# Row sums of a 16384 x 1024 matrix: the first 2048 rows on 64 partitions, the last 2048 as one group

## The chip, the cores and the metric

The kernel runs on one core of a Trainium2 chip. The metric is the device time of one execution in microseconds (us), as the median of several runs. The core has a vector engine (DVE in the profile), a scalar engine (ACT), a GpSimd engine (POOL), a tensor engine that this kernel leaves idle, a sync engine (SP) that only issues transfers, and 16 DMA engines that carry the transfers between the memory outside (DRAM) and the buffer on the core, which has 128 partitions.

## The reference

```
batch, seq, dim = 32, 512, 1024
x: (32, 512, 1024) float32, normally distributed
return np.sum(x, axis=-1).astype(np.float32)        # (32, 512)
```

So 16384 rows of 1024 numbers (4 KB each, 64 MB in all) are read, and one sum for each row (64 KB in all) is written.

## The kernel before

**Tiling.** The rows are cut into eight groups of 2048. A group puts 16 consecutive rows (`BIG = 16`) on each of the 128 partitions: that is the view `x_g[g, p, j, d]` (L120). One partition's share of a group is therefore 64 KB that lie in one piece in DRAM. Input tiles hold a whole group, and the pool has three of them (L133), so the load of a fourth tile waits until the sums over the first one are done.

**Sums.** `vec` (L140) is one instruction of the vector engine that sums all the rows of a tile on each partition. `halves` (L153) is another form for one row: it adds the two halves of the row and sums the result. `act` (L166) has the scalar engine copy one row into a tile nobody reads, with the row's sum on the side. All sums land in the tile `sums`, one column per row of a partition.

**The helper `rows(t, a, n, j, n_act, pairs)`** (L177) loads `n` rows per partition with one transfer on SP's queue and gives the last `n_act` of them to the scalar engine and the others to the vector engine, as one `vec` or, with `pairs`, as one `halves` per row.

**Order of the work.** The schedule is manual: each engine does its instructions in the order in which they are written.

1. The first 7 rows per partition of the *last* group (`FIRST = 7`, L199), 3.5 MB, summed by one `vec`. This is the very first transfer: `issue_first_load_at_entry` (L10) moves the first load of SP's queue ahead of the barrier with which the program starts.
2. Groups 0 to 5, each with one load of 8 MB and one `vec`. The load of group 1 is held (`hold`, L145, adds a wait) until the first 7 rows have been summed.
3. Group 6 with one load; its rows are shared, 9 for `halves` and 7 for `act`.
4. The other 9 rows per partition of the last group in falling pieces: 6 rows, 2 rows, and one row that is itself cut at column 560 (`pieces = (560, 464)`). The two parts of that row are loaded into neighbouring places (`part`, `whole`); the sum of the first part is written into a column ahead of the second part, so that the second `halves` gives the sum of the row.
5. Two stores. The sums of groups 0 to 6 go out on the scalar engine's queue, held until the transfer of 2 rows (`two`) has landed. The sums of the last group go out on SP's queue after everything (L227).

`order_waits` (L31) puts the waits of an instruction in order, and `wait_for_the_store_at_the_clear` (L55) has the last store awaited by GpSimd's last clearing of semaphores instead of by SP.

Of the kernel before, what the change touches and what calls it, by code (L numbers as in the profile page):

```python
# [100 lines left out]
@with_exitstack  # L101
def kernel(
    ctx: ExitStack,
    tc: tile.TileContext,
    x: bass.AP,
    out: bass.AP,
):
    nc = tc.nc
    nc.at_finalize(issue_first_load_at_entry)
    nc.at_finalize(order_waits)  # L110
    nc.at_finalize(wait_for_the_store_at_the_clear)
    fp32 = mybir.dt.float32
    P = 128
    batch, seq, dim = x.shape
    rows = batch * seq
    J = rows // P
    BIG = 16


    x_g = x.flatten_outer_dims().rearrange("(g p j) d -> g p j d", p=P, j=BIG)  # L120
    out_v = out.rearrange("b s -> (b s)").rearrange("(g p j) -> p g j", p=P, j=BIG)

    def rows_from(j, n):
        return x_g[j // BIG, :, j % BIG : j % BIG + n, :]

    last = J // BIG - 1
    FIRST = 7
    pieces = (560, 464)  # L130

    with (
        tc.tile_pool(name="in", bufs=3) as inpool,  # L133
        tc.tile_pool(name="unread", bufs=4, space=bass.MemoryType.PSUM) as upool,
        tc.tile_pool(name="stage", bufs=1) as stpool,
        tc.manual_schedule(),
    ):
        sums = stpool.tile([P, J], fp32)

        def vec(dst, src):  # L140
            return nc.vector.tensor_reduce(  # L141
                out=dst, in_=src, axis=mybir.AxisListType.X, op=mybir.AluOpType.add
            )

        def hold(inst, until, reason):  # L145
            tc.add_manual_dep(
                inst.ins,
                until.ins.name,
                mybir.DependencyInfo(mybir.DependencyClass.Sync, mybir.DependencyReason.DATA),
                reason=reason,  # L150
            )

        def halves(dst, src):  # L153
            n = src.shape[-1] // 2
            return nc.vector.tensor_tensor_reduce(  # L155
                out=src[:, :n],
                in0=src[:, :n],
                in1=src[:, n:],
                scale=1.0,
                scalar=0.0,  # L160
                op0=mybir.AluOpType.add,
                op1=mybir.AluOpType.add,
                accum_out=dst,
            )

        def act(dst, src, n):  # L166
            unread = upool.tile([P, dim], fp32)
            nc.scalar.activation(  # L168
                out=unread[:, :n],
                in_=src,  # L170
                func=mybir.ActivationFunctionType.Copy,
                accum_out=dst,
            )

        sums_of = []

        def rows(t, a, n, j, n_act, pairs=False):  # L177
            nv = n - n_act
            block = t[:, a * dim : (a + n) * dim].rearrange("p (n d) -> p n d", d=dim)
            load = nc.sync.dma_start(out=block, in_=rows_from(j, n))  # L180
            if pairs:
                for q in range(nv):
                    sums_of.append(halves(sums[:, j + q : j + q + 1], block[:, q, :]))
            else:
                sums_of.append(vec(sums[:, j : j + nv], block[:, :nv, :]))
            for q in range(nv, n):
                act(sums[:, j + q : j + q + 1], block[:, q, :], dim)
            return load

        def store(eng, g0, g1):  # L190
            return eng.dma_start(
                out=out_v[:, g0:g1],
                in_=sums[:, g0 * BIG : g1 * BIG].rearrange("p (g j) -> p g j", j=BIG),
            )


        j = last * BIG
        t = inpool.tile([P, BIG * dim + 4], fp32)
        rows(t, 0, FIRST, j, 0)  # L199
        first = sums_of[-1]  # L200
        for g in range(last):
            t = inpool.tile([P, BIG * dim + 4], fp32)
            if g < last - 1:
                load = rows(t, 0, BIG, g * BIG, 0)
            else:
                rows(t, 0, BIG, g * BIG, 7, pairs=True)
            if g == 1:
                hold(load, first, "no descriptors of later loads while the first ones start")

        t = inpool.tile([P, BIG * dim + 4], fp32)  # L210
        rows(t, FIRST, 6, j + FIRST, 2, pairs=True)
        two = rows(t, FIRST + 6, 2, j + FIRST + 6, 1, pairs=True)
        a = BIG - 1

        j += a
        c, width = pieces
        whole = t[:, a * dim + c : BIG * dim + 2]
        nc.vector.memset(whole[:, width + 1 :], 0.0)  # L220
        part = t[:, a * dim : a * dim + c]
        nc.sync.dma_start(out=part, in_=rows_from(j, 1)[:, 0, :c])  # L222
        nc.sync.dma_start(out=whole[:, 1 : width + 1], in_=rows_from(j, 1)[:, 0, c:])
        hold(store(nc.scalar, 0, last), two, "its packets come behind those of the loads")
        halves(whole[:, :1], part)
        halves(sums[:, j : j + 1], whole)
        store(nc.sync, last, last + 1)  # L227


# [28 lines left out]
```

## Time and profile before

| what | value |
|---|---|
| time, median of 3 runs | 161.67 us (161.61 to 161.68) |
| span of the profiled execution, first to last instruction | 159.9 us |
| median time less that span (the profiled execution's own time is not given separately) | 1.8 us |
| vector engine busy | 120.6 us, 75%, 40 instructions |
| scalar engine busy | 12.0 us, 8%, 21 instructions |
| read from DRAM / written | 67.11 MB / 0.07 MB, 420 GB/s over the span |
| SP's queue (q1): packets, MB, share of the 16 DMA engines' time | 1872, 67.12, 97.7% |
| the scalar engine's queue (q10) | 912, 0.06, 0.4% |
| all packets; of these under 512 B / 2 KB / 8 KB | 2784; 1248 / 1376 / 1504 |

How to read it: the DMA engines are busy for nearly the whole span and the others are not, so what the kernel can lose or win lies where the DMA engines are not yet, or no longer, at work. A packet is one piece that one DMA engine moves. A load of a whole group is 128 packets of 64 KB, one for each partition, and 16 further packets of a few bytes that report its completion. The counts come out so: 12 loads of 128 packets are 1536, the stores move 1024 packets of 64 B, and 14 transfers report with 16 packets each (224); 1024 + 224 is the 1248 under 512 B, and with 1536 the whole 2784.

### The profile page before, as it was taken

Reading aid. Unit: us, or ns where it says so; the run is one execution under the profiler, and the core shown is the slowest. Engines: PE = TensorE matmul, PEld = TensorE weight load, DVE = VectorE, ACT = ScalarE, POOL = GpSimd, SP = SyncE. Lnnn points to the kernel's source line nnn. Section 1 sums busy time; section 2 is a strip of 40 time slices with the busy share of each in tenths; the row PEclk is TensorE's granted clock in tenths of the full one; section 3 lists DMA queues with packets and bytes.
Section 4 is the critical chain, followed back from the end, with each engine's and each line's share of the span. In section 5 each row is a group of like instructions: output and inputs, shape, how many; then the busy total and the mean of one; then the engine's idle time right before and its main releaser. Section 6 shows DMA issues by size and latency. Waiting matters only on the chain.

```text
span 159.9 us, 132 instructions
## 1 busy us (share of the span) xinstructions
DVE 120.6 (75%) x40; ACT 12.0 (8%) x21; POOL 0.2 (0%) x4
## 2 busy tenths in 40 slices
DVE  0029600499985999779995899949999499994955
ACT  3000000000000000000000000000000000003993
POOL 0000000000000000000000000000000000000000
DMA  8899899799699699699699699799898996996994
GB/s 308 380 492 525 361 426 525 328 459 525 295 492 525 262 525 525 262 525 525 262 525 508 279 525 476 312 525 410 377 525 361 426 525 262 525 525 289 400 384 124
DMA packets 2784, 67.18 MB, mean 420 GB/s; under 512 B 1248, under 2 KB 1376, under 8 KB 1504
## 3 DMA queue, kind: packets, MB, share of 16 engines
q1 hardware_dynamic: 1872, 67.12, 97.7%
q10 hardware_dynamic: 912, 0.06, 0.4%
HBM read 67.11 MB, written 0.07 MB: 420 GB/s over the span
## 4 chain that ended last, share of the span: by engine, by line
DMA 71%; DVE 27%; SPq 1%; issue 0%; DVEq 0%
DMA t<-in_x_dram 71%; DVE sums L141 26%; SPq L180 0%; SPq L222 0%; DVE t L155 0%; DVEq L253 0%
## 5 line engine op out<-in xcount | busy, mean ns | idle before, releaser
L141 DVE TENSOR_REDUCE sums<-t 128x16 f32<-128x16384 f32 (+1 forms) x7 | 110.9, 15848 | 33.4 <-DMA t<-in_x_dram 33.4
L168 ACT ACTIVATE unread<-t 128x1024 f32<-128x1024 f32 x10 | 10.1, 1013 | 144.7 <-DMA t<-in_x_dram 144.7
L155 DVE CUSTOM_DVE_ANT_0 t<-t 128x512 f32<-128x512 f32 (+2 forms) x16 | 9.6, 654 | 4.1 <-DMA t<-in_x_dram 4.0
L168 ACT ACTIVATION_READ_ACCUMULATOR unread<-t 128x1 f32 x10 | 1.9, 188 | 0.0
L168 ACT ACT_TABLE_LOAD x1 | 1.3, 1283 | 0.8 <-PEq L242 0.8
L155 DVE DVE_READ_ACCUMULATOR2_ANT sums<- 128x1 f32 x15 | 1.2, 81 | 0.0
L242 POOL MEMSET const-bfloat16-1.0<- 128x1 bf16 x1 | 0.1, 102 | 0.0
L242 POOL MEMSET const-uint8-127<- 128x1 uint8 x1 | 0.1, 102 | 0.0
L242 POOL MEMSET const-float32-1.0<- 128x1 f32 x1 | 0.1, 99 | 0.0
L242 POOL MEMSET const-float32-0.0<- 128x1 f32 x1 | 0.1, 98 | 0.2 <-issue 0.2
L155 DVE DVE_READ_ACCUMULATOR2_ANT t<- 128x1 f32 x1 | 0.1, 83 | 0.0
L220 DVE MEMSET t<- 128x1 f32 x1 | 0.1, 59 | 0.0
## 6 DMA issues: line engine op xcount, KB each, us to landing
t<-in_x_dram SPq DMA_DIRECT2D x1, 3584.0 KB, 11.0
t<-in_x_dram SPq DMA_DIRECT2D x1, 3072.0 KB, 28.9
t<-in_x_dram SPq DMA_DIRECT2D x1, 1024.0 KB, 31.0
t<-in_x_dram SPq DMA_DIRECT2D x1, 280.0 KB, 31.2
t<-in_x_dram SPq DMA_DIRECT2D x1, 232.0 KB, 31.3
t<-in_x_dram SPq DMA_DIRECT2D x7, 40.8
out_dram<-sums ACTq DMA_DIRECT2D x1, 56.0 KB, 2.1
out_dram<-sums SPq DMA_DIRECT2D x1, 8.0 KB, 1.4
```

The costliest lines, as they stand in the source:

```text
L141: return nc.vector.tensor_reduce(out=dst, in_=src, axis=mybir.AxisListType.X, op=mybir.AluOpType.add)
L155: return nc.vector.tensor_tensor_reduce(out=src[:, :n], in0=src[:, :n], in1=src[:, n:], scale=1.0, scalar=0.0, op0=mybir.AluOpType.add, op ...
L168: nc.scalar.activation(out=unread[:, :n], in_=src, func=mybir.ActivationFunctionType.Copy, accum_out=dst,)
L220: nc.vector.memset(whole[:, width + 1 :], 0.0)
L242: nc = _bacc.Bacc("TRN2", target_bir_lowering=False, num_devices=1)
```

## The change

The rows that used to be group 0 (the first 2048) are now read in another shape. They are put on the 64 partitions 32 to 95 in two "lines" of 1024 rows, again 16 consecutive rows per partition (view `x_s[l, q, j, d]`). Line 0 comes with four loads ("quarters"), the r-th of which takes the partitions 32 + r, 36 + r, 40 + r and so on: 16 partitions, 1 MB, each. Line 1 comes with one load of 64 partitions, which is held until the first quarter has landed. Of each line the vector engine sums the partitions 32 to 63 with one `vec`, and the scalar engine the partitions 64 to 95 with 16 `act`. The load of group 1 is held until the fourth quarter has landed.

The last group is no longer begun at the start. It comes at the end, whole, in pieces of 8, 5, 2 and 1 rows per partition, the one row cut as before. Of the 8 rows the scalar engine gets 3, of the 5 rows 2, of the 2 rows 1.

`sums` gets 16 columns more, since the two lines take 16 columns each on half of the partitions. Their sums are written by a store of their own on the scalar engine's queue, ahead of that of groups 1 to 6.

```diff
-    last = J // BIG - 1
-    FIRST = 7
+    LOW, HALF, Q = 32, 64, 32
+    x_s = x.flatten_outer_dims()[: P * BIG].rearrange("(l q j) d -> l q j d", l=2, j=BIG)
+    out_s = out.rearrange("b s -> (b s)")[: P * BIG].rearrange("(l q j) -> q l j", l=2, j=BIG)
+    last = G - 1
...
-        sums = stpool.tile([P, J], fp32)
+        sums = stpool.tile([P, J + BIG], fp32)
+        def at(g):
+            return (g + 1) * BIG
...
+        def line(t):
+            return t[LOW : LOW + HALF, : BIG * dim].rearrange("p (n d) -> p n d", d=dim)
+
+        def sum_line(t, c):
+            block = t[:, : BIG * dim].rearrange("p (n d) -> p n d", d=dim)
+            a = slice(LOW, LOW + Q)
+            vec(sums[a, c : c + BIG], block[a])
+            a = slice(LOW + Q, LOW + HALF)
+            for q in range(BIG):
+                act(sums[a, c + q : c + q + 1], block[a, q, :], dim, a)
...
-        j = last * BIG
         t = inpool.tile([P, BIG * dim + 4], fp32)
-        rows(t, 0, FIRST, j, 0)
-        first = sums_of[-1]
-        for g in range(last):
+        quarters = [
+            nc.sync.dma_start(out=line(t)[r::4], in_=x_s[0, r::4]) for r in range(4)
+        ]
+        sum_line(t, 0)
+        t = inpool.tile([P, BIG * dim + 4], fp32)
+        second = nc.sync.dma_start(out=line(t), in_=x_s[1])
+        hold(second, quarters[0], "no descriptors of later loads while the first ones start")
+        sum_line(t, BIG)
+
+        for g in range(1, last):
             t = inpool.tile([P, BIG * dim + 4], fp32)
             if g < last - 1:
-                load = rows(t, 0, BIG, g * BIG, 0)
+                load = rows(t, g, 0, BIG, 0)
             else:
-                rows(t, 0, BIG, g * BIG, 7, pairs=True)
+                rows(t, g, 0, BIG, 7, pairs=True)
             if g == 1:
-                hold(load, first, "no descriptors of later loads while the first ones start")
+                hold(load, quarters[3], "no descriptors of later loads while the first ones start")
 
         t = inpool.tile([P, BIG * dim + 4], fp32)
-        rows(t, FIRST, 6, j + FIRST, 2, pairs=True)
-        two = rows(t, FIRST + 6, 2, j + FIRST + 6, 1, pairs=True)
+        rows(t, last, 0, 8, 3, pairs=True)
+        rows(t, last, 8, 5, 2, pairs=True)
+        two = rows(t, last, 13, 2, 1, pairs=True)
...
-        hold(store(nc.scalar, 0, last), two, "its packets come behind those of the loads")
+        first = nc.scalar.dma_start(
+            out=out_s,
+            in_=sums[LOW : LOW + HALF, : 2 * BIG].rearrange("p (l j) -> p l j", j=BIG),
+        )
+        hold(first, two, "its packets come behind those of the loads")
+        hold(store(nc.scalar, 1, last), two, "its packets come behind those of the loads")
         halves(whole[:, :1], part)
-        halves(sums[:, j : j + 1], whole)
+        halves(sums[:, at(last) + a : at(last) + a + 1], whole)
         store(nc.sync, last, last + 1)
```

The helper `rows` now takes the group and the row in it instead of two offsets, and `act` takes the partitions it works on.

More of the change, by code (lines that the diff above doesn't have):

```diff
@@ L117 @@
     BIG = 16
+    G = J // BIG
     x_g = x.flatten_outer_dims().rearrange("(g p j) d -> g p j d", p=P, j=BIG)
     out_v = out.rearrange("b s -> (b s)").rearrange("(g p j) -> p g j", p=P, j=BIG)
-    def rows_from(j, n):
-        return x_g[j // BIG, :, j % BIG : j % BIG + n, :]
-    last = J // BIG - 1
-    FIRST = 7
+    LOW, HALF, Q = 32, 64, 32
+    x_s = x.flatten_outer_dims()[: P * BIG].rearrange("(l q j) d -> l q j d", l=2, j=BIG)
+    out_s = out.rearrange("b s -> (b s)")[: P * BIG].rearrange("(l q j) -> q l j", l=2, j=BIG)
+    last = G - 1
     pieces = (560, 464)
@@ L164, in halves, with act @@
             )
-        def act(dst, src, n):
+        def act(dst, src, n, on=slice(None)):
             unread = upool.tile([P, dim], fp32)
             nc.scalar.activation(
-                out=unread[:, :n],
+                out=unread[on, :n],
                 in_=src,
@@ L173, in act, with rows @@
             )
-        sums_of = []
-        def rows(t, a, n, j, n_act, pairs=False):
+        def rows(t, g, j, n, n_act, pairs=False):
             nv = n - n_act
-            block = t[:, a * dim : (a + n) * dim].rearrange("p (n d) -> p n d", d=dim)
-            load = nc.sync.dma_start(out=block, in_=rows_from(j, n))
+            block = t[:, j * dim : (j + n) * dim].rearrange("p (n d) -> p n d", d=dim)
+            load = nc.sync.dma_start(out=block, in_=x_g[g, :, j : j + n, :])
+            c = at(g) + j
             if pairs:
                 for q in range(nv):
-                    sums_of.append(halves(sums[:, j + q : j + q + 1], block[:, q, :]))
+                    halves(sums[:, c + q : c + q + 1], block[:, q, :])
             else:
-                sums_of.append(vec(sums[:, j : j + nv], block[:, :nv, :]))
+                vec(sums[:, c : c + nv], block[:, :nv, :])
             for q in range(nv, n):
-                act(sums[:, j + q : j + q + 1], block[:, q, :], dim)
+                act(sums[:, c + q : c + q + 1], block[:, q, :], dim)
             return load
+        def line(t):
[7 more added lines that the diff above has]
+                act(sums[a, c + q : c + q + 1], block[a, q, :], dim, a)
         def store(eng, g0, g1):
@@ L192, in store @@
                 out=out_v[:, g0:g1],
-                in_=sums[:, g0 * BIG : g1 * BIG].rearrange("p (g j) -> p g j", j=BIG),
+                in_=sums[:, at(g0) : at(g1)].rearrange("p (g j) -> p g j", j=BIG),
             )
-        j = last * BIG
         t = inpool.tile([P, BIG * dim + 4], fp32)
-        rows(t, 0, FIRST, j, 0)
-        first = sums_of[-1]
-        for g in range(last):
+        quarters = [
[7 more added lines that the diff above has]
+        for g in range(1, last):
             t = inpool.tile([P, BIG * dim + 4], fp32)
             if g < last - 1:
-                load = rows(t, 0, BIG, g * BIG, 0)
+                load = rows(t, g, 0, BIG, 0)
             else:
-                rows(t, 0, BIG, g * BIG, 7, pairs=True)
+                rows(t, g, 0, BIG, 7, pairs=True)
             if g == 1:
-                hold(load, first, "no descriptors of later loads while the first ones start")
+                hold(load, quarters[3], "no descriptors of later loads while the first ones start")
         t = inpool.tile([P, BIG * dim + 4], fp32)
-        rows(t, FIRST, 6, j + FIRST, 2, pairs=True)
-        two = rows(t, FIRST + 6, 2, j + FIRST + 6, 1, pairs=True)
+        rows(t, last, 0, 8, 3, pairs=True)
+        rows(t, last, 8, 5, 2, pairs=True)
+        two = rows(t, last, 13, 2, 1, pairs=True)
         a = BIG - 1
-        j += a
         c, width = pieces
@@ L221 @@
         part = t[:, a * dim : a * dim + c]
-        nc.sync.dma_start(out=part, in_=rows_from(j, 1)[:, 0, :c])
-        nc.sync.dma_start(out=whole[:, 1 : width + 1], in_=rows_from(j, 1)[:, 0, c:])
-        hold(store(nc.scalar, 0, last), two, "its packets come behind those of the loads")
+        nc.sync.dma_start(out=part, in_=x_g[last, :, a, :c])
+        nc.sync.dma_start(out=whole[:, 1 : width + 1], in_=x_g[last, :, a, c:])
+        first = nc.scalar.dma_start(
[4 more added lines that the diff above has]
+        hold(store(nc.scalar, 1, last), two, "its packets come behind those of the loads")
         halves(whole[:, :1], part)
-        halves(sums[:, j : j + 1], whole)
+        halves(sums[:, at(last) + a : at(last) + a + 1], whole)
         store(nc.sync, last, last + 1)
```

## The prediction

> **What bounds the kernel now.** I read the page first, then the vector engine's timeline, the busy times by stretch, the chain that ended last, and the start once more in short stretches.
>
> The vector engine's timeline (start, duration, what, in brackets the idle time before it and what ended it):
>
> ```profile
> 11.03 7.62 DVE L141 TENSOR_REDUCE sums<-t 128x7 f32<-128x7168 f32 x1 [11.03 <-DMA t<-in_x_dram]
> 30.34 17.22 DVE L141 TENSOR_REDUCE sums<-t 128x16 f32<-128x16384 f32 x1 [11.69 <-DMA t<-in_x_dram]
> 49.69 17.22 DVE L141 TENSOR_REDUCE sums<-t 128x16 f32<-128x16384 f32 x1 [2.14 <-DMA t<-in_x_dram]
> ```
>
> Every reduce waits for its load. They follow one another by 19.35 us and take 17.22, so a group of 8 MiB costs 19.35 us of transfer (433.5 GB/s) and the engine has 2.13 us to spare in each. The stretches say the same of the DMA engines (columns: stretch, length, busy DVE, ACT, POOL with counts, clock, DMA share, GB/s):
>
> ```profile
> 11.00:30.30 19.30, 7.62 (x1) 0.00 (x0) 0.00 (x0) 1.00 1.00 435
> 88.40:107.70 19.30, 17.22 (x1) 0.00 (x0) 0.00 (x0) 1.00 1.00 435
> 146.50:159.90 13.40, 9.66 (x33) 10.71 (x20) 0.00 (x0) 1.00 0.82 328
> ```
>
> The share is 1.00 in the middle. Time is lost only at the two ends. Of the chain that ended last (start, length, what) the ends matter:
>
> ```profile
> 0.00 11.01 DMA t<-in_x_dram
> 11.01 0.02 issue
> ...
> 126.33 31.29 DMA t<-in_x_dram
> 157.62 0.07 issue
> 157.69 0.40 DVE t L155
> ```
>
> 64 MiB at 19.35 us per 8 MiB are 154.80 us, and the last load lands at 157.62: 2.82 us are lost up to there. The first load, 7/16 of a group, should take 8.47 us and lands at 11.01, so 2.54 of the 2.82 lie at the start, and 0.28 in all the rest. After the landing come 2.26 us (last half sum, store, clearing) up to 159.88. The median is 161.67, 1.79 more than the span. I make the sum against the span and add 1.79.
>
> Now the start (packets are counted in the stretch where they begin; one is 28672 bytes here):
>
> ```profile
> 0.00:1.00 1.00, 0.00 (x0) 0.22 (x1) 0.20 (x4) 1.00 0.00 0
> 1.00:1.10 0.10, 0.00 (x0) 0.10 (x1) 0.00 (x0) 1.00 6.40 1720
> 1.10:1.30 0.20, 0.00 (x0) 0.20 (x1) 0.00 (x0) 1.00 3.79 1004
> 1.30:1.60 0.30, 0.00 (x0) 0.30 (x1) 0.00 (x0) 1.00 0.92 287
> 1.60:2.60 1.00, 0.00 (x0) 0.46 (x1) 0.00 (x0) 1.00 0.00 0
> 2.60:2.80 0.20, 0.00 (x0) 0.00 (x0) 0.00 (x0) 1.00 2.32 1004
> 2.80:3.05 0.25, 0.00 (x0) 0.00 (x0) 0.00 (x0) 1.00 2.39 1032
> 4.70:5.30 0.60, 0.00 (x0) 0.00 (x0) 0.00 (x0) 1.00 1.85 765
> ```
>
> GB/s times length over 28672 gives packets: 6 + 7 + 3 = 16, one for each DMA engine, beginning anywhere between 1.0 and 1.6; then 7 + 9 = 16 second ones between 2.6 and 3.05. Share times length times 16 over the count gives their mean duration: 1.71, 1.73 and 1.47 us for the first packets by the time they begin (1.67 over all), 1.06 for the second ones. The 16 packets of 4.70 to 5.30 took 1.11. So a first packet costs 0.61 us too much, the last engine is on its second packet only at 3.05, which is as if it had begun at 3.05 - 1.06 = 1.99 and lost nothing, and some 0.1 us more goes in the packets up to 6.5 (in the stretches 3.65 to 4.15, 4.70 to 5.30 and 5.80 to 6.50 the mean excess is 0.02, 0.05 and 0.01). 1.99 + 0.1 = 2.09; the other 0.45 of the 2.54 lie between the last data and the report of the landing.
>
> **The change part by part.**
>
> *The first load.* 16 packets of 64 KB instead of 128 of 28 KB: one per DMA engine. It removes nothing that must be transferred. It can only move the two losses above: when the last engine begins, and how long its first packet takes beyond its bytes. Before, 128 descriptors are written for the first load and, issued at 0.78 us, 128 more for group 0 while the first packets run. After, it is 16 and then 48 (the three other quarters, at 328 ns to some 440 ns per issue on SP, from 0.78 to about 2 us). Nothing in the trace shows a load of 16 packets, so I bound it. Best: the last engine begins at 1.0, when the first one did, with the excess of the late starters, 1.47 - 1.06 = 0.41: 1.41 in place of 2.09, a gain of 0.68. Worst: the excess isn't a latency but belongs to the bytes; then 0.61 becomes 0.61 x 64/28 = 1.39, a loss of 0.78. I take a latency, since the late starters had less of it at the same size, and a value inside: begin at 1.1, by when six of the sixteen had begun, excess 0.5, no excess later: 1.6 in place of 2.09, gain 0.49. The other quarters are issued by 2 us and needed at 1.1 + 0.5 + 2.42 (a 64 KB packet at 19.35/8) = 4.0, so there is no gap. The 2 us are also before any other need of SP.
>
> *Line 1* is held until the first quarter lands (about 4.4), needed at 1.6 + 4 x 2.42 = 11.3: cover of nearly 7 us for an issue that took 1.0 us from instruction to first packet. *Group 1* is held until the fourth quarter lands, about 11.7, needed at 21.0: cover 8 us. Queued behind it on SP are only later loads, which wait for buffers anyway.
>
> *Half the partitions.* Every load of before has 128 partitions, and the middle rows give 433.5 GB/s for them; no row has 64 or 16. From above, half the partitions could run at half the rate (line 1: 4 MiB in 19.35 us instead of 9.68); from below, the same rate. I take the same, the row being the nearest there is, and keep the other end as a rival. A rule of the Trainium skill speaks against the change: the page "SBUF — State Buffer", section "Door 1: The DMA port swizzle", says that partitions 0 to 63 reach only half of 16 ports, with 196 GB/s against 328 for 128 partitions. By that measured ratio the two lines would need 8 MiB in 32.4 us, 13 more, and the time would be near 174. The same section's formula puts partitions 32 to 63 on one half of the ports and 64 to 95 on the other, though, so that this very range reaches all 16, and by that nothing is added.
>
> *Sums of the lines.* A partition still has 16 rows, so `vec` costs 17.22 us on 32 partitions if width doesn't matter, and 16 `act` follow at the 1.04 us at which the ACT rows follow one another: 16.6. Width below 128 isn't in the trace; the cover bounds what it could cost. With landings at 11.8 + 9.68 = 21.5 for line 1 and then every 19.35 (40.8, 60.2, 79.5, 98.9, 118.2, 137.6), the vector engine runs 11.8 to 29.0, 29.0 to 46.2, then groups 1 to 3 back to back until 97.9, and has caught up by group 4. What its lateness could delay are the buffers: group 2 needs line 0's tile (free at 29.0, needed by 40 less an issue of 1), group 3 line 1's (46.2 against 59), group 4 the next (63.5 against 78). The least cover is 10 us, so 0.
>
> *The end.* The last group's 16 rows now all come there. Group 6 lands at 137.6 instead of 146.5; its 9 `halves` (5.5 us) and 7 `act` (7.3) are done before the 8 rows land. Five rows land where six landed, at 153.85 less the gain, and cost 3 `halves` rather than 4, done 0.6 us earlier; but the next two rows land at 156.34 either way, so nothing is won. From there the instructions are the same: 0.
>
> *Reports and stores.* Loads go from 12 to 16; a report packet takes a DMA engine about 9 ns: 4 x 9 = 0.04 us loss. The scalar engine now issues two stores. The first keeps the time of the old one (156.45, 0.41 us), the second follows 0.45 later and so lands at about 156.90 + 2.1 = 159.0 instead of 158.6; SP awaits it before the closing barrier, for which some 0.6 us are needed, up to 159.6; the last store lands at 159.56. So it comes out even; between 0 and 0.1, I take 0.05.
>
> Sum: 159.88 - 0.49 + 0.04 + 0.05 = 159.48; with 1.79, **161.3 us**. A measurement of this kernel can tell about 0.2% (0.32 us) from no change, so this is just outside.
>
> **The rivals.**
>
> *No change.* Start spread and excess belong to the cold DMA engines and the memory, not to the number of descriptors. For it: the first 16 packets of the last store begin within 0.02 us of one another although 128 are queued, so writing descriptors isn't obviously slow. Against: three engines began up to half a microsecond late here. Then 0 + 0.09: 161.75; all that is within 0.2% I count here.
>
> *Slower, by bytes.* The first packet runs slowly over its whole length, at the start of the stream. Price 0.78 + 0.09: 162.5. It decides once the excess of the first 16 packets is over 0.61 + 0.32 - 0.09 = 0.84 us. Against it stands the shorter excess of the late starters.
>
> *Slower, half the partitions.* Line 1 at half the rate, +9.68: 171.3; it decides as soon as line 1 runs below 97% of the rate of the groups.
>
> *It doesn't do what it says*: the quarter isn't 16 packets on 16 engines but fewer engines carry several each. Then line 0 takes a multiple of 9.68; this I count with the last one.
>
> **How the numbers follow.** Forecast (faster by over 0.32) 0.46, no change 0.31, slow by bytes 0.14, half the rate 0.09. The range runs from the best start, 161.67 - 0.68 + 0.09 = 161.1, or 160.9 if the excess shrinks to half that of the late starters, to the slower first packet, 162.5; only the last rival (and a little on each side) stays out. The forecast's own range is 160.9 to 161.35.
>
> **What would show it.** First reduce at 11.8 to 11.9 (the sum without a gain gives 2.54 + 9.68 = 12.2); the next landing 9.7 later, though the second reduce starts at once after the first, at 29.0; from group 4 on reduces wait for DMA again. First 16 packets in under 0.3 us and with 2.9 us mean. Page: 2864 packets, 1328 under 512 B; DVE about 132 us busy, ACT about 48. Wrong: a first reduce at 12.2 or later, a DMA share below 1.00 between 12 and 21 us, or a reduce of groups 4 or 5 that doesn't wait for DMA.

## The result: slower by 1.2%

The changed kernel takes 163.67 us (median of 4 runs, 163.48 to 163.96), the kernel before 161.67: ratio 1.0122, 95% interval 1.0103 to 1.0141. The forecast was 161.3, and its range ended at 162.5, so the change moved the time the other way and beyond the range. The profiled execution of the changed kernel has a span of 161.6 us, 1.76 more than before, and took 163.83.

### The profile page after: what moved, and what is told of

Read it like the earlier page. It is cut to its first block, busy times and chain, and to the rows that moved or that the text cites. A ratio compares the mean times of both kernels' runs of the same rounds, so it can differ in the third digit from the quotient of the medians.

```text
span 161.6 us, 225 instructions
## 1 busy us (share of the span) xinstructions
DVE 132.5 (82%) x48; ACT 48.6 (30%) x91; POOL 0.2 (0%) x4
## 2 busy tenths in 40 slices
DMA packets 2865, 67.18 MB, mean 416 GB/s; under 512 B 1328, under 2 KB 1456, under 8 KB 1584
## 4 chain that ended last, share of the span: by engine, by line
DMA 53%; DVE 43%; SPq 2%; issue 0%; DVEq 0%
DMA t<-in_x_dram 53%; DVE sums L145 43%; SPq L182 1%; SPq L213 1%; SPq L239 0%; DVE t L159 0%; DVEq L145 0%; DVEq L275 0%
## 5 line engine op out<-in xcount | busy, mean ns | idle before, releaser
L145 DVE TENSOR_REDUCE sums<-t 128x16 f32<-128x16384 f32 (+1 forms) x7 | 120.2, 17212 | 17.0 <-DMA t<-in_x_dram 16.9
L172 ACT ACTIVATE unread<-t 32x1024 f32<-32x1024 f32 (+1 forms) x45 | 45.2, 1006 | 96.5 <-DMA t<-in_x_dram 96.5
L159 DVE CUSTOM_DVE_ANT_0 t<-t 128x512 f32<-128x512 f32 (+2 forms) x20 | 12.2, 662 | 9.9 <-DMA t<-in_x_dram 9.8
L172 ACT ACTIVATION_READ_ACCUMULATOR unread<-t 32x1 f32 (+1 forms) x45 | 8.3, 184 | 0.0
```

The source lines that it names most:

```text
L145: return nc.vector.tensor_reduce(out=dst, in_=src, axis=mybir.AxisListType.X, op=mybir.AluOpType.add)
L159: return nc.vector.tensor_tensor_reduce(out=src[:, :n], in0=src[:, :n], in1=src[:, n:], scale=1.0, scalar=0.0, op0=mybir.AluOpType.add, op ...
L172: nc.scalar.activation(out=unread[on, :n], in_=src, func=mybir.ActivationFunctionType.Copy, accum_out=dst,)
```

## The profile after

The vector engine's timeline (start, duration, what; the first line covers five reduces that follow one another):

```profile
13.65 85.84 DVE L145 TENSOR_REDUCE sums<-t 32x16 f32<-32x16384 f32 x5 [13.65 <-DMA t<-in_x_dram]
100.64 17.22 DVE L145 TENSOR_REDUCE sums<-t 128x16 f32<-128x16384 f32 x1 [1.16 <-DMA t<-in_x_dram]
119.99 17.22 DVE L145 TENSOR_REDUCE sums<-t 128x16 f32<-128x16384 f32 x1 [2.13 <-DMA t<-in_x_dram]
```

The first reduce starts at 13.65, where 11.8 was forecast and 12.2 would have been no gain. After that the engine runs without a pause until it has caught up with group 4 at 100.64, and from there every reduce waits for its load again. That part went as worked out. The DMA engines' stretches say why it does not matter:

```profile
22.00:41.00 19.00, 19.00 (x2) 19.00 (x39) 0.00 (x0) 1.00 0.96 414
100.60:119.90 19.30, 17.22 (x1) 0.00 (x0) 0.00 (x0) 1.00 1.00 435
148.90:161.60 12.70, 6.65 (x23) 6.57 (x12) 0.00 (x0) 1.00 0.74 292
```

The middle is as before (the 0.96 is where a stretch cuts packets that are counted by their start). The chain that ended last:

```profile
2.41 11.12 DMA t<-in_x_dram
...
119.69 39.23 DMA t<-in_x_dram
158.91 0.05 issue
158.97 0.40 DVE t L159
```

The last load lands at 158.91 instead of 157.62: 1.29 us later. From there to the end of the span it takes 161.64 - 158.91 = 2.73 us, before 2.26: another 0.47. What lies outside the span was 1.78 to 2.23 us in the four runs (median 2.08), in the runs of the kernel before 1.73 to 1.83: some 0.3 more, with a spread that is larger than that. 1.29 + 0.47 + 0.3 = 2.06 is the 2.0 that the median moved.

The start, in short stretches (one packet is now 65536 bytes):

```profile
0.00:1.30 1.30, 0.00 (x0) 0.00 (x0) 0.20 (x4) 1.00 0.00 0
1.30:1.60 0.30, 0.00 (x0) 0.00 (x0) 0.00 (x0) 1.00 5.12 1748
1.60:2.40 0.80, 0.00 (x0) 0.00 (x0) 0.00 (x0) 1.00 1.69 655
4.20:5.00 0.80, 0.00 (x0) 0.00 (x0) 0.00 (x0) 1.00 2.85 1065
5.00:5.70 0.70, 0.00 (x0) 0.00 (x0) 0.00 (x0) 1.00 0.76 281
6.90:7.40 0.50, 0.00 (x0) 0.00 (x0) 0.00 (x0) 1.00 3.21 1311
7.40:8.40 1.00, 0.00 (x0) 0.00 (x0) 0.00 (x0) 1.00 0.93 393
12.00:13.30 1.30, 0.00 (x0) 0.00 (x0) 0.00 (x0) 1.00 1.88 807
```

Read as in the prediction: no packet begins before 1.3 (before: 1.0); 8 begin by 1.6 and 8 up to 2.4. They took 3.07 and 2.70 us, 2.89 on the mean, 0.47 over the 2.42 of their bytes. Of the second packets 13 begin by 5.0, and three only between 5.0 and 5.7; they took 2.81 and 2.84, still 0.4 too much. The ten third packets that begin at 6.9 to 7.4 took 2.57, and six more begin only between 7.4 and 8.4. The landing waits for the last engine and not for the mean one: the slowest of the second packets took 3.39 us in the trace, and the last of the third ones begins at 8.31. The 16 of line 1 (12.0 to 13.3) took 2.44: 64 partitions run at full rate. So the loss is one of the first 8 us.

The end, in the timeline and in what SP's queue waited for:

```profile
157.72 0.70 ACTq L241 DMA_DIRECT2D out_dram<-sums  x1
158.51 0.54 ACTq L205 DMA_DIRECT2D out_dram<-sums  x1
159.40 0.35 SPq L205 DMA_DIRECT2D out_dram<-sums  x1
```

```profile
SPq L275 <- DMA out_dram<-sums: 0.8, 1, 0.8
```

The first store on the scalar engine's queue takes 0.70 us to issue (the one of before 0.41), so the second goes out 0.80 us behind the start of the first and lands at 160.65. SP waits 0.8 us for it, and that wait was not there before.

## The experiments

Each is an edit of the changed kernel unless another is named. "Loss at the start" is the start of the first reduce less its transfer at 19.35 us per 8 MiB: 11.03 - 8.47 = 2.56 before, 13.65 - 9.68 = 3.97 after (0.1 of it, because a reduce that waits for four loads starts 0.1 us after the landing at 13.53). Two theories stood at first: the shape of the loads (fewer than 128 partitions) costs, or the three further issues do; a third, from the prediction, was that first packets of 64 KB run slowly over their whole length.

**one_load**: line 0 in one load, line 1 not held.

```diff
-        quarters = [
-            nc.sync.dma_start(out=line(t)[r::4], in_=x_s[0, r::4]) for r in range(4)
-        ]
+        quarters = [nc.sync.dma_start(out=line(t), in_=x_s[0])]
...
-        hold(second, quarters[0], ...)
```

> Line 0 in one load of 64 partitions in place of the four quarters; line 1 is issued right behind it, without the hold. The changed kernel loses some 1.3 us at the start (its last load lands at 158.91 us, before at 157.62) and some 0.5 us at the end. Theory 'shape': a load of fewer than 128 partitions costs SP more to issue (586 ns against 376) and its packets begin later and further apart (1.37 to 2.16 us against 1.02 to 1.55). Then one load of 64 partitions still begins near 1.37, the last load lands at 158.5 or later and the time stays within 0.3 us of the changed kernel's 163.67. Theory 'several issues': the engines are held up because three more loads are issued while the first packets run. Then the second packets follow at once on all engines, line 0 has landed by 12.6 instead of 13.53, and the time is 0.8 to 1.0 us lower. Theory 'long first packets': 64 KB first packets run slowly over their whole length; then nothing changes, since they are as long.

162.69 us (1.0062, 1.0039 to 1.0084): 1.0 us comes back. The first reduce starts at 12.49, a loss of 2.81. In its short stretches:

```profile
1.30:2.40 1.10, 0.00 (x0) 1.10 (x1) 0.00 (x0) 1.00 2.70 953
4.20:5.00 0.80, 0.00 (x0) 0.00 (x0) 0.00 (x0) 1.00 3.02 1311
```

The 16 first packets begin as late as in the changed kernel and took 2.97 us, but all 16 second ones follow by 5.0 and took 2.42. SP needs 0.60 us for this first issue as well (0.59 with the quarters, 0.38 before). So the shape costs the late beginning, 0.25 us of loss, and something that only the quarters have (or the hold of line 1, which is gone here too) costs 1.1 at the start: line 0 lands at 13.53 with them, at 12.47 here. Not all of that reaches the end. The last load lands at 158.26, only 0.65 us earlier than in the changed kernel, because from line 1's landing to group 1's it takes 19.78 us here and 19.33 there. A packet of 8 KB with instructions lies in that stretch (see pad_dve), but in the changed kernel too, so what costs the 0.45 here is not shown. The rest of the 1.0 lies outside the span, with 1.76 to 1.82 us here.

**halves**: line 0 in two loads of 32 partitions.

```diff
-            nc.sync.dma_start(out=line(t)[r::4], in_=x_s[0, r::4]) for r in range(4)
+            nc.sync.dma_start(out=line(t)[r::2], in_=x_s[0, r::2]) for r in range(2)
```

> Line 0 in two loads of 32 partitions (every second one) in place of four of 16. Theory 'shape': the first issue takes near 586 ns again and the first packets begin near 1.37 us; only one more issue in place of three, so little changes, within 0.3 us of 163.67. Theory 'several issues': the loss falls with the number of issues behind the first, by about two thirds of what one load alone gains, so 0.5 to 0.7 us below 163.67. Theory 'long first packets': no change.

172.54 us (1.0675, 1.0659 to 1.0691), which none of the theories had (the name is that of the run and not of the function `halves`). Its stretch with the second 16 packets:

```profile
5.90:7.00 1.10, 0.00 (x0) 0.00 (x0) 0.00 (x0) 1.00 4.45 953
```

16 packets of 4.90 us: twice 2.42. All 64 packets of line 0 are about as long, and the first reduce starts at 22.36, 9.87 us later than in one_load, which is nearly the difference of the times (9.85). This is the prediction's rival of half the rate, only not in the kernel it was meant for: 16 partitions a step of 4 apart and 64 in a row run at full rate, 32 a step of 2 apart at half. By the formula in the Trainium skill's page "SBUF — State Buffer", section "Door 1: The DMA port swizzle", the first 16 partitions of such a load (32, 34, ... 62) lie on 8 of 16 ports. That would give half the rate if these 16 were written at one time, but by the same reading the first 16 of one_load's line 0 (32 to 47) lie on 4 ports, and those packets ran at full rate. So why step 2 runs at half the rate is not shown.

**last_whole**: the other part of the change alone. Group 0 comes whole on 128 partitions, the last group at the end; one store.

```diff
-        quarters = [...]        # and both lines
-        for g in range(1, last):
+        for g in range(last):
...
+            if g == 2:
+                hold(loads[2], loads[0], ...)
```

> Only the other part of the change: group 0 comes whole on 128 partitions as the first load, groups 1 to 6 as before (the load of group 2 held until group 0 has landed), the last group at the end in pieces of 8, 5, 2 and 1 rows, and one store on the scalar engine's queue. First packets are 64 KB here too, but 128 of them, all from one load. Theories 'shape' and 'several issues': the start is that of before, first packets begin by 1.02 to 1.55 us with an excess of about 0.6 us over 2.42, and the time is 161.67 within 0.2 us. Theory 'long first packets': their mean is 2.42 x 1.67/1.06 = 3.8 us, the last load lands 0.8 us later than before, and the time is about 162.5.

162.30 us (1.0042, 1.0029 to 1.0055). The first reduce starts at 21.95, a loss of 2.60: as before.

```profile
0.90:1.30 0.40, 0.00 (x0) 0.40 (x1) 0.00 (x0) 1.00 6.97 2294
1.30:2.00 0.70, 0.00 (x0) 0.70 (x1) 0.00 (x0) 1.00 0.49 187
4.00:4.80 0.80, 0.00 (x0) 0.00 (x0) 0.00 (x0) 1.00 3.02 1311
```

14 of the 64 KB packets begin by 1.3, the 16 took 3.13 us on the mean, an excess of 0.71 and not 1.39, and the second ones 2.42. The theory of long first packets falls. The span is 160.0 us, within 0.2 of before; the missing 0.4 us lies outside it: 2.14 to 2.25 us in seven runs.

**store_early**: the store of the lines' sums is issued right behind `sum_line(t, BIG)` and not held.

```diff
         sum_line(t, BIG)
+        first = nc.scalar.dma_start(out=out_s, ...)
...
-        hold(first, two, "its packets come behind those of the loads")
```

> The changed kernel with the store of the lines' sums issued as soon as the scalar engine has done line 1 and the vector engine's sums are there (about 48 us) instead of behind the loads at the end. Theory: the second of two stores on the scalar engine's queue is issued 0.80 us after the first (158.51 after 157.72) and lands at 160.65, so that SP is let into the closing barrier 0.7 us late; with one store left at the end the closing is as before, 2.25 us from the last landing to the end of the span instead of 2.7, and the time is 0.4 to 0.5 us below 163.67. Rival: the tail is long for another reason (more loads whose semaphores SP must await, a longer program); then the span ends 2.6 to 2.7 us after the last landing as now, and the time stays.

163.30 us, 0.37 below the changed kernel, but with intervals that overlap (1.0081 to 1.0127 here, 1.0103 to 1.0141 there), so the reading goes by the end of the span. The last load lands at 158.87 and the span ends at 161.08, 2.21 us later, as before the change. In the list of SP's waits the 0.8 us for a store are gone, and the last two waits are back to those of the kernel before:

```profile
SPq L274 <- PEq L274: 0.9, 2, 0.7
```

So the second store costs 0.5 us at the end.

Next, why the quarters cost what one load does not.

**second_later**: `hold(second, quarters[1], ...)` in place of `quarters[0]`.

> The changed kernel with the load of line 1 held until the second quarter has landed (8.66 us) instead of the first (5.04). Theory 'issue of line 1': three engines begin their second packet only at 5.28 to 5.58 us because 64 descriptors are issued at 5.06; then those gaps go, the 16 packets of the second quarter begin within 4.3 to 4.8 us, line 0 lands at about 12.7 instead of 13.53, and the time falls by 0.6 to 0.9 us. Theory 'quarters themselves' (either their issues at 1.23 to 2.99 us or their shape): the late second packets stay, line 0 lands at 13.2 to 13.6, and the time stays within 0.3 us of 163.67.

163.64 us, first reduce at 13.63.

```profile
4.20:5.00 0.80, 0.00 (x0) 0.00 (x0) 0.00 (x0) 1.00 3.53 1311
```

The three late beginnings are gone (the 16 second packets begin within 4.28 to 4.89), but they still took 2.82 us on the mean and up to 3.52. Line 1's issue is not the cause.

**four_64**: line 0 in four loads of four rows on all 64 partitions.

```diff
-            nc.sync.dma_start(out=line(t)[r::4], in_=x_s[0, r::4]) for r in range(4)
+            nc.sync.dma_start(out=line(t)[:, r : r + 4], in_=x_s[0, :, r : r + 4])
+            for r in range(0, BIG, 4)
```

> Line 0 still in four loads, but each takes four of the 16 rows on all 64 partitions (packets of 16 KB, four to an engine in each load) in place of all rows on 16 partitions; the rest as changed. Theory 'number of issues': four issues of 500 to 600 ns at the start cost what they did, line 0 lands near 13.5 us. Theory 'shape': the loss belongs to 16 partitions a step of 4 apart; then line 0 lands as with one load of 64 partitions, at 12.5 us, and the time is within 0.3 us of the changed kernel's less 1.0, about 162.7.

163.66 us, first reduce at 13.63: 16 partitions a step apart do as badly as 64 in a row. Here again it is the second load's packets that are long, from 4.4 to 8 us.

**four_128**: last_whole with group 0 in four loads of four rows on 128 partitions.

```diff
+                    fours = [
+                        nc.sync.dma_start(out=block[:, r : r + 4], in_=x_g[0, :, r : r + 4, :])
+                        for r in range(0, BIG, 4)
+                    ]
```

> As last_whole, but group 0 comes in four loads of four rows on all 128 partitions, and group 1 is held until the first of them has landed. Theory 'number of issues': the landing of group 0 goes from 21.93 to 22.5 us or later and the time rises by 0.5 us or more. Theory 'shape' (fewer than 128 partitions is what costs): it stays within 0.2 us of last_whole's 162.30, the issues taking 330 to 440 ns each as elsewhere.

161.87 us (1.0014, 1.0004 to 1.0023); group 0 lands at 21.97 us. Four issues cost nothing here. But a load of four rows on 128 partitions is 2 MB, and its packets last until 6.4 to 6.9 us, so this left open whether shape or an early end decides.

**two_64**: line 0 in two loads of eight rows on 64 partitions (the edit is shown against four_64).

```diff
-            for r in range(0, BIG, 4)
+            for r in range(0, BIG, 8)        # and r : r + 8
```

> Line 0 in two loads of eight rows on all 64 partitions (four_64 has four loads, one_load one; line 0 landed at 13.51 and 12.47). Theory 'each further issue costs the same' (1.04 / 3 = 0.35 us each): line 0 lands at 12.8 us, the time is about 163.0 to 163.2. Theory 'any second load during the first packets costs all of it': 13.3 to 13.6 us and 163.6. Theory 'only the third and fourth do': 12.5 us and 162.7.

162.86 us, first reduce at 12.57: no loss beyond that of one load. **eight_four_four** and **four_twelve** (the same with pieces of 8, 4, 4 and of 4, 12 rows) separate the number of issues from the moment at which the second load takes over:

> Line 0 in three loads of 64 partitions with 8, 4 and 4 rows. Theory 'third and fourth issue': packets between 4 and 8 us run slowly though they belong to the first load for the most part, and line 0 lands at 12.8 to 13.5 us. Theory 'early end of the first load': 12.5 us, full rate throughout.

> Line 0 in two loads of 64 partitions, the first with 4 rows, the second with 12. Theory 'third and fourth issue': as two_64, line 0 lands at 12.5 us, the packets from 4.4 to 8 us run at full rate. Theory 'early end of the first load': as four_64, those packets are 10 to 30% long and line 0 lands at 13.2 to 13.6 us.

Three issues with a late hand-over: first reduce at 12.57 (162.77 us). Two issues with an early one: 13.43 (163.44 us, two runs). So it is not their number. The stretches of four_twelve and of two_64 in which their second load's packets begin:

```profile
4.20:5.50 1.30, 0.00 (x0) 0.18 (x1) 0.00 (x0) 1.00 1.52 618
6.20:7.70 1.50, 0.00 (x0) 1.49 (x5) 0.00 (x0) 1.00 1.24 524
```

```profile
6.80:7.40 0.60, 0.00 (x0) 0.00 (x0) 0.00 (x0) 1.00 2.04 874
```

Packets of 48 KB, 16 in each stretch (and one of 16 KB in the first), begin at 4.2 to 5.5 and 6.2 to 7.7 and took 1.93 and 1.86 us, where 1.81 is their bytes' time; their starts spread over 0.9 and 1.3 us, and the slowest took 2.94. In two_64 (32 KB, from 6.8 on) the 16 packets took 1.22 us, where 1.21 is due, and began within 0.6. The starts of line 0 side by side, all on partitions 32 to 95:

| run | line 0 comes as | second load takes over at | first reduce |
|---|---|---|---|
| one_load | one load | (none) | 12.49 |
| changed kernel | four loads of 16 partitions | 4.3 | 13.65 |
| four_64 | 4, 4, 4, 4 rows on 64 | 4.4 | 13.63 |
| four_twelve | 4, 12 rows on 64 | 4.5 | 13.43 |
| two_64 | 8, 8 rows on 64 | 6.9 | 12.57 |
| eight_four_four | 8, 4, 4 rows on 64 | 6.7 | 12.57 |

**two_fourteen** and **short_wide** ask whether an early hand-over costs with the other shape: last_whole with group 0 in pieces of 2 and 14 rows, and four rows of line 0 on 64 partitions with group 1 on 128 behind them.

> As last_whole, but group 0 comes in two loads of 2 and 14 rows on 128 partitions; the first one is through at about 4.3 us (8 packets of 8 KB to an engine), the second was issued at 0.78. Theory 'early end': the packets from 4.3 to 8 us are 5 to 20% longer than their bytes and group 0 lands at 22.6 us or later (21.93 in last_whole). Theory 'short shape': full rate and a landing at 21.8 to 22.0.

> First four rows of line 0 on 64 partitions as in four_twelve, then group 1 on 128 partitions, then the other 12 rows of line 0 and line 1; only the start is looked at (the order costs waits later). Theory 'early end of a first load': group 1's first packets, from 4.4 to 8 us, are 3 to 10% longer than 2.42 us on average, as the second load's are in four_twelve (1.93 and 1.86 us in place of 1.81). Theory 'two short loads in succession': they follow at 2.42 us.

Neither loses: two_fourteen has group 0 landed at 21.76 and takes 161.73 us (1.0004, 0.9994 to 1.0014); in short_wide (one run, 165.99 us, its later order costs waits) group 1's first 16 packets begin at 4.4 to 4.8 and took 2.42 us. Not run was the mixed case, a first load on 128 partitions with one on 64 taking over early. **mid_quarters** has group 0 first and the lines second (164.37 us, two runs); only the start is read, since the order costs waits later.

> Group 0 comes first, whole, on 128 partitions, and it is group 1 that comes as two lines on 64 partitions, line 0 of them in four quarters; these are issued from 0.8 to 3 us as in the changed kernel, while group 0's packets run, and their own packets run from about 22 us on. (The sums of group 0 and of the lines are stored early.) Theory 'issues': issuing loads of fewer than 128 partitions slows whatever packets run 2 to 6 us after; then group 0's packets take more than 2.42 us on average between 3 and 8 us and group 0 lands at 22.5 us or later instead of 21.93. Theory 'packets': the quarters' own packets are slow; then group 0 is as in last_whole and the quarters' packets take 2.5 to 2.8 us near 22 to 30 us. Theory 'cold start': neither is slow, since the loss needs both short loads and DMA engines that have just started; group 0 lands at 21.9, the lines' 16 packets follow one another by 2.414 us.

```profile
20.90:21.60 0.70, 0.00 (x0) 0.00 (x0) 0.00 (x0) 1.00 3.47 1498
23.30:24.00 0.70, 0.70 (x1) 0.00 (x0) 0.00 (x0) 1.00 3.47 1498
```

Group 0 lands at 21.91, and the quarters' packets follow at 16 per 2.4 us, 2.43 us each. **mid_lead** puts the issue of line 0, in one load, shortly before its turn in mid-stream:

> As mid_quarters (group 0 first, on 128 partitions; then the lines), but group 0 comes as 13 and 3 rows, and line 0 in one load of 64 partitions that is held until the 13 rows have landed, near 18.3 us; its packets take over from group 0's at about 21.4, some 3 us after the issue, as the second load did in four_twelve. Theory 'too soon after the issue': its first packets are 5 to 20% longer than 2.42 us or late, and line 0 lands at 32.2 us or later. Theory 'cold start': they follow without a gap at 2.42 us and line 0 lands at 31.5 to 31.7 us, as in mid_quarters (31.60).

Line 0 lands at 32.37 (one run, 162.59 us), but because group 0 itself is late (22.69). From there it is 9.68 us, full rate, and the line's packets took 2.42 us although the first began 2.6 us after the start of the issue. A short notice in itself does not lengthen the load's own packets. Of group 0's delay 0.3 us is there when its 13 rows land (18.61); the last three rows then take 4.08 us where their bytes take 3.63:

```profile
17.00:18.30 1.30, 0.00 (x0) 0.00 (x0) 0.00 (x0) 1.00 0.65 274
18.30:19.40 1.10, 0.76 (x1) 0.00 (x0) 0.00 (x0) 1.00 0.99 391
```

Their packets (12 KB) that begin before 18.3 took 0.46 us, those right behind it 0.50, and line 0's issue lies at 18.63 to 19.21. Whether the issue of a load on 64 partitions slows another load's packets there was not tested; in mid_quarters, where such issues lie beside group 0's first packets, group 0 landed in time.

**pad_dve**: last_whole with 16 memsets of one column on the vector engine at the start.

> last_whole with 16 more instructions on the vector engine (a memset of one column of a scratch tile, at the start, while the engine is idle). They lie beside the first load, so the span should stay at 160.0 us. Theory: what lies outside the span depends on how long the engines' programs are; then device time less span moves away from last_whole's 2.14 to 2.25 us by 0.1 or more. Rival: it belongs to something else, such as the transfers or the last group's pieces; then it stays at 2.14 to 2.25.

162.38 us, hardly other than last_whole, but differently composed: outside the span 1.78 to 1.82 us instead of 2.14 to 2.25, and the span 160.4 to 160.7 instead of 159.9 to 160.6. Its page has a line that last_whole's has not:

```profile
q14 instruction: 1, 0.01, 0.0%
```

It is one packet of 8 KB, at 151.8 us in the trace, among the last loads, and the last load lands at 158.46 instead of 157.79. The changed kernel has one such packet too, at 36.3 us. So with sixteen tiny instructions more there are 0.4 us less outside the span and about half a us more inside it; that the packet is what delays the loads fits its place, and is not shown.

**two_mended**: one_load and store_early together.

> The changed kernel with both mendings: line 0 in one load, and the store of the lines' sums issued early. If the terms add (1.0 us from the start, 0.48 from the end of the span), the time is 162.69 - 0.48 = 162.2, between the kernel before (161.66) and one_load; what is left is 0.27 us from the later start of a load of 64 partitions, and some 0.3 us for a packet of 8 KB with instructions that is fetched in the middle of the loads, near 36 us. If the second store's delay is hidden in one_load, it stays at 162.6 to 162.7.

162.37 us; 1.0031 (1.0020 to 1.0041) against the runs of before on the same chip, which is 0.50 us over them, where 0.54 was expected. The terms add. In the profiled executions the last load lands 0.69 us later than before (158.31): 0.31 of it is there when line 0 lands (12.53), and 0.36 comes between the landings of line 1 and group 1, which are 19.71 us apart, as in one_load.

**lean**: four_128 with group 6's and the 8 rows' sums on the vector engine in one reduce each.

```diff
-                rows(t, g, 0, BIG, 7, pairs=True)
+                rows(t, g, 0, BIG, 7)
...
-        rows(t, last, 0, 8, 3, pairs=True)
+        rows(t, last, 0, 8, 3)
```

> An attempt at a faster kernel: four_128 (group 0 on 128 partitions in four loads of four rows, last group whole at the end) with fewer instructions: the 9 rows of group 6 and the first 5 rows of the last group that the vector engine sums go into one reduce each instead of 9 and 5 single sums. four_128 has a span of 159.95 us, like before, but 1.94 us outside it against 1.78. Theory: what is outside grows where the program's end needs one more fetch of instructions; with a shorter program it is 1.78 again, and the time 161.6 to 161.75, level with before. Rival: what is outside doesn't depend on the length, and the time stays at 161.87; or the longer reduces (9.7 and 5.4 us) delay the pieces behind them, and it rises by 0.2 us or more.

1.0000 (0.9988 to 1.0011), 161.77 us where before had 161.87 in the same rounds. Outside the span it is 1.74 to 1.82 again, four_128's 1.89 to 1.98 are gone. No kernel here beats the one before.

## Why the prediction was wrong

**The first load** is the step that failed. It bounded the moment at which the last engine begins by the rows of before, from 1.0 us on, and took 1.1: "begin at 1.1, by when six of the sixteen had begun". In place of that no packet begins before 1.3: the first one begins at 1.37 and not at 1.02, and the 16th at 2.16. The issue for 16 or 64 partitions takes SP 0.50 to 0.60 us where the traces of before showed 0.33 to 0.44; for the first issue that is 0.21 of the 0.35 us (0.59 against 0.38), and the rest is not explained. The bound came from loads of 128 partitions and was used as if it held for any. The excess of 0.5 us came out (0.47 measured; 0.55 in one_load), but it was paid from a later beginning. one_load shows this term alone: 0.25 us lost, not 0.49 gained.

**"So there is no gap"** failed in the same paragraph. The quarters were all issued by 2.99 us and not by 2, but still before they were needed; what the step did not have is that the packets of the second quarter run 16% too long on the mean, and the slowest by 0.97 us, which the landing waits for. A loss of 0.9 to 1.1 us at line 0's landing came in every run that had two loads of fewer than 128 partitions in succession at the start with a hand-over at 4.3 to 4.5 us, and in none with a hand-over at 7 us or with a second load on 128. Whether the first load's width matters was not tested. What it is that does this stays open.

**The rivals.** Slow by bytes had the sign, but its mechanism is refuted by last_whole and four_64. Half the rate is refuted for the changed kernel by line 1's 2.44 us: of the two readings of the port rule in the prediction, the formula held for this range and the measured ratio did not carry over to it. That the quarter is not 16 packets on 16 engines is refuted by the 16 packets that begin between 1.37 and 2.16 and overlap. No change is refuted by one_load's late beginning.

**The end.** The second store was given 0.05 us, from an issue of 0.41 and a distance of 0.45. It is 0.70 and 0.80. By the prediction's own figures the closing chain had some 0.35 us to spare (159.56 - 158.6 - 0.6, an estimate); they were used up, and 0.47 came on top. The row it was sized by was a store from 128 partitions; the store from 64, like the loads from fewer than 128, takes longer to issue.

**The 1.79 us outside the span** were taken as fixed. In the kernel before they are (1.73 to 1.83 in all its runs whose span is given). In the changed kernel they vary from 1.78 to 2.23 in four runs, and four_64 had 1.82 three times and 2.19 once; pad_dve and lean show that a few instructions more or less move it. The trace of the changed kernel has one packet behind the end of the span, 1.98 us after it (a list of the window from 161.7 to 164.2 us):

```profile
q14 instruction: 1, 0.01, 1.1%
```

The five profiled executions with such a packet (the changed kernel, store_early, second_later, four_64, mid_quarters) had 2.05 to 2.19 us outside the span. Those without one whose time is given had 1.78 to 1.95, all but last_whole, which had 2.19. So the packet goes with the longer time in most programs, and that it is the cause is not shown.

**What held:** the sums of the lines (17.20 us on 32 partitions, 1.00 for an activation), their cover and the catching up at group 4, the last pieces, the full rate on partitions 32 to 95, and the page's counts (2864 packets and one of instructions, 1328 small ones, DVE 132.5 us, ACT 48.6).

## What to carry to other kernels

A bound is only as good as the row it comes from: a row of another shape bounds nothing, and the price of an issue belongs to the shape just as that of a transfer does. When the DMA engines set the time from end to end, little is left to win at the start (the prediction's own best case was 0.68 us; the most that a run here won was two_fourteen's 0.13, group 0 landing 2.41 us behind its transfer time where 2.54 were lost before), and a transfer of an unfamiliar shape that is put there can cost more than that; it was safer in mid-stream, where the same four quarters ran at full rate behind a load of 128 partitions. And before a second store is put at the end of a queue, count its issue at its own shape into the chain that closes the program.

## What the runs showed of the hardware that was not expected

- An issue from SP takes 0.33 to 0.49 us for 128 partitions (a program's first one 0.37 to 0.38) and 0.47 to 0.60 for 16, 32 or 64 (the first one 0.55 to 0.60); from the scalar engine, 0.40 to 0.41 for a store of 128 partitions (0.54 to 0.63 right behind one of 64) and 0.69 to 0.70 for one of 64. A first load's packets begin at 1.0 us with 128 partitions and at 1.35 to 1.4 with fewer.
- 32 partitions a step of 2 apart, from 32 on, took 4.9 us for a 64 KB packet; 16 a step of 4 apart and 64 in a row over the same range took 2.42 to 2.43.
- Programs that differ by 16 small instructions (last_whole and pad_dve) differ by 0.4 us in what lies outside the span. The longer one has a packet of 8 KB on the queue of instructions among its last loads, and its last load lands 0.67 us later.
